# z = h @ w_in as seven products in place of eight, in two halves of the tokens, with q, k and v kept in DRAM

## The chip, the cores and the metric

The kernel runs on one core of a Trainium2 chip. A core has TensorE (PE) for matmuls, VectorE (DVE), ScalarE (ACT) and GpSimd (POOL) for work on whole tiles, and SyncE (SP), whose queue issues nearly all DMAs here. Each engine takes its own instructions in order and waits for the others by semaphores. The metric is device time in microseconds of one execution.

## What is computed

One layer of a decoder trunk over 2048 prompt tokens and 8 sample tokens, in float32. The heart is one wide product, and all branches hang on it:

```python
def _branches_in(x, c, w_c, b_c, w_in, b_in):
    mod = c @ w_c + b_c
    shift, scale, gate = jnp.split(mod, 3, axis=-1)
    h = x * (1.0 + scale[:, None]) + shift[:, None]
    z = h @ w_in + b_in
    return gate, jnp.split(z, SPLIT_POINTS, axis=-1)
...
        gate_p, (q, k, v, ga, glu, gb, ma, mb) = _branches_in(x_p, c_prompt, w_c, b_c, w_in, b_in)
...
        o_attn = _combine_groups(outs, lses)
        u = _glu(glu)
...
        conv_out = _conv_tail(u_ext, conv_w, conv_b, conv_norm_g, conv_norm_b)
...
    a = (o_attn.reshape(B, T, ATTN_OUT).astype(x.dtype) * jax.nn.silu(ga)) @ w_pa
    b = (conv_out * jax.nn.silu(gb)) @ w_pb
    y = (jax.nn.sigmoid(ma) * a + jax.nn.sigmoid(mb) * b) @ w_o
    return _layer_norm(ALPHA * x + gate[:, None] * y, ln_g, ln_b)
```

h has 1024 channels and w_in 8704 columns, 68 tiles of 128: 36 for q, k and v (12 heads of 128), 4 for the attention gate, 8 for the convolution's gated input, 4 for its gate, 16 for the merge gates. The heads stand in three groups with dilations 1, 4 and 16; a query sees its own and the previous block of keys within its residue class (group three has one block of keys only). The groups of a head slot are combined by their softmax denominators. The convolution has 31 taps per channel, then a LayerNorm. The samples attend to caches of keys and values in DRAM.

## The kernel before

**Matmuls in three parts.** w_in and h are each split into a high and a low part in a faster matmul format (ACT copies the high part, POOL or DVE subtracts it for the low part: `w_split`, lines 133 to 139, and `h_step`), and each product is high x high, high x low and low x high (`products`, line 322). The split h of all tokens stays in SBUF for the whole kernel.

**Units.** A tile of 128 columns of w_in is worked in five units of tokens, three of 512, one of 256 and one of 264 with the samples (`UNITS`, `unit`), each 24 matmuls into one PSUM bank of tag `pm` (three buffers). ACT or DVE then evacuates it (`ev_qkv`, `ev_merge`, `ev_ga`, `ev_glu`, `ev_gb`). q, k and v go to SBUF slots, permuted so that a residue class is contiguous.

**Order.** `seq` is written out by hand: one merge gate tile beside which h is made, then v, k, q head by head, an attention gate after each head slot but the last, the convolution's inputs spread among merge gates, last the convolution's gates. After most units `tick` issues what was put off, one step of a background `lane` (a generator), and steps of `conv_lane` as long as a clock kept for DVE lies behind one kept for PE. The lane holds, in turn, turning v into rows (`v_rows`), k rows for the output (`k_rows`) and `attention`: scores of a batch of blocks, mask and maximum on DVE, exponentials on ACT, turns on PE, values on PE, rows to DRAM (`orow`). These three stages are shifted by one step each, so that a step issues the values of batch s-2, the turns of s-1 and the scores of s. A step follows every 5.5 us unit, more or less. Later the lane holds the samples' attention (`s_attn`, line 886 the keys, 942 to 944 the values), the residual gate (`gate_rows`, line 971) and the convolution's norm. The combination of a head slot (`combiner`) is worked inside the units of its gate tile (`ga_tile`), two pieces at a time from four or five buffers.

**Output.** The output weights are loaded and split beneath the last two gate tiles. Then for eight chunks of tokens come the two branch products (line 1297), the merge, the product with w_o (line 1340) and the LayerNorm.

## Time and profile before

| | us |
|---|---|
| median of 3 runs | 2282.08 (2281.2 to 2283.14) |
| span of the profiled execution | 2280.6 |
| first instruction to the end of the first tile of z, about | 88.7 |
| q, k, v and attention, up to about | 1144 |
| samples, convolution, up to about | 1545 |
| remaining gates, up to | 1889.5 |
| output | 391.1 |

The page doesn't give the profiled execution's own time beside its span; the span is 1.5 us below the median of the runs. To read the rows: a matmul's duration in the trace contains its way through the array, and the next one starts before it ends, so the pace is read from start to start, or from the chain of critical work, which merges neighbours. "PE L322" is a matmul of z; "PEld" the load of its weights, which overlaps. An engine's number in a stretch is its busy time there.

### The profile page before, as it was taken

The page shows a single profiled execution, that of the slowest core. Times are in us where ns is not written, and L with a number is a line of the kernel's source. Part 1 is how long each engine was busy: PE and PEld are TensorE (multiplying, and loading weights), DVE is VectorE, ACT ScalarE, POOL GpSimd, SP SyncE. Part 2 cuts the span into 40 slices and gives each one's busy share as a digit, 9 for nine tenths or more (in the row PEclk, how much of TensorE's full clock was granted, in tenths as well). Part 3 has the DMA queues.
Part 4 walks back from the last instruction along what each step waited for, and adds up shares of the span by engine and source line. Part 5 has one row for each costly group of instructions (what it writes and reads, how often), then busy time and mean ns, then how long its engine had stood idle before and what let it go on. Part 6 is the DMA issues. An engine that isn't in the chain of part 4 may idle for free.

```text
span 2280.6 us, 30595 instructions
## 1 busy us (share of the span) xinstructions
PE 2191.2 (96%) x12633; PEld 1893.6 (83%) x12633; DVE 1038.2 (46%) x1473; ACT 625.4 (27%) x1227; POOL 529.6 (23%) x380
## 2 busy tenths in 40 slices
PE   6999999999999999999999797989999999999998
PEld 4888888888888888888888675878888888888886
DVE  4402211211512215122245999998934545554556
ACT  2323332333413334133341111221134332111110
POOL 2501001010001001010012549341122135322232
PEclk9999999999999999999999899999999999999999
DMA  7301112111320113111223532312222356334220
GB/s 255 112 21 35 39 49 56 30 34 43 120 59 22 39 50 112 53 33 39 77 87 108 157 90 78 96 52 84 70 70 80 98 185 221 110 121 130 93 95 30
DMA packets 198888, 190.16 MB, mean 83 GB/s; under 512 B 9355, under 2 KB 172991, under 8 KB 198741
## 3 DMA queue, kind: packets, MB, share of 16 engines
q1 hardware_dynamic: 198425, 187.76, 26.4%
q8 instruction: 99, 1.62, 0.3%
q10 hardware_dynamic: 324, 0.45, 0.1%
q14 instruction: 40, 0.33, 0.0%
HBM read 130.37 MB, written 58.31 MB: 83 GB/s over the span
## 4 chain that ended last, share of the span: by engine, by line
PE 75%; DVE 14%; issue 3%; DMA 1%; ACT 1%; POOL 1%; SPq 0%; POOLq 0%; DVEq 0%; ACTq 0%
PE ps_pm L322 52%; DVE slot L75 9%; PE py L1340 8%; PE pab L1297 5%; PE ps_S L433 3%; PE ps_U L473 2%; PE ps_PT L459 1%; PE ps_U L471 1%; DVE slot L71 1%; PE ps_PT L515 1%; DMA slot<-orow 1%; DVE st L1236 0%; DMA stg<-smp_d 0%; DVE ev L75 0%; DVE th L71 0%
## 5 line engine op out<-in xcount | busy, mean ns | idle before, releaser
L138 POOL TENSOR_TENSOR wL<-raw,wH 128x1024 fp32r<-128x1024 f32 x68 | 182.3, 2681 | 1150.8 <-ACT wH L137 1109.9
L322 PE MATMUL ps_pm<-h3H,wH 128*128 128x256 f32 (+1 forms) x1088 | 314.5, 289 | 0.0
L322 PE MATMUL ps_pm<-h3L,wH 128*128 128x256 f32 (+1 forms) x1088 | 309.0, 284 | 0.9 <-POOL h3L L295 0.9
L322 PE MATMUL ps_pm<-h3H,wL 128*128 128x256 f32 (+1 forms) x1088 | 307.9, 283 | 0.0
L322 PE MATMUL ps_pm<-h1H,wH 128*128 128x512 f32 x544 | 221.5, 407 | 0.0
L322 PE MATMUL ps_pm<-h2H,wH 128*128 128x512 f32 x544 | 219.4, 403 | 0.0
L322 PE MATMUL ps_pm<-h0H,wH 128*128 128x512 f32 x544 | 218.1, 401 | 0.0
L322 PE MATMUL ps_pm<-h1H,wL 128*128 128x512 f32 x544 | 215.8, 397 | 0.0
L322 PE MATMUL ps_pm<-h1L,wH 128*128 128x512 f32 x544 | 215.6, 396 | 0.0
L322 PE MATMUL ps_pm<-h2L,wH 128*128 128x512 f32 x544 | 214.3, 394 | 1.1 <-POOL h2L L295 1.1
L322 PE MATMUL ps_pm<-h0H,wL 128*128 128x512 f32 x544 | 214.1, 394 | 0.7 <-POOL wL L138 0.7
L322 PE MATMUL ps_pm<-h2H,wL 128*128 128x512 f32 x544 | 214.4, 394 | 0.0
L322 PE MATMUL ps_pm<-h0L,wH 128*128 128x512 f32 x544 | 213.5, 393 | 0.0
L83 DVE COPY Uo<-ps_U 128x256 f32<-128x256 f32 (+1 forms) x76 | 37.6, 495 | 382.0 <-PE ps_U L473 368.9
L322 PEld LDWEIGHTS ps_pm<-h3H,wH 128*128 128x128 f32 x1088 | 206.7, 190 | 5.0 <-issue 1.9
L322 PEld LDWEIGHTS ps_pm<-h3L,wH 128*128 128x128 f32 x1088 | 206.7, 190 | 3.0 <-POOL h3L L295 1.7
L322 PEld LDWEIGHTS ps_pm<-h3H,wL 128*128 128x128 f32 x1088 | 206.0, 189 | 0.0
L364 ACT ACTIVATE slot<-ps_pm,bT 128x512 f32<-128x512 f32 (+1 forms) x120 | 102.5, 854 | 313.4 <-PE ps_pm L322 312.5
L75 DVE SCALAR_TENSOR_TENSOR slot<-slot,cwT,slot 128x2048 f32<-128x2048 f32 x60 | 178.9, 2981 | 1.4
L75 DVE SCALAR_TENSOR_TENSOR slot<-u,cwT,slot 128x2048 f32<-128x2048 f32 x60 | 167.5, 2791 | 1.6
L75 DVE SCALAR_TENSOR_TENSOR X<-tab,ps_S 128x512 f32<-128x512 f32 (+1 forms) x80 | 52.3, 653 | 173.7 <-PE ps_S L433 171.9
L322 PEld LDWEIGHTS ps_pm<-h1H,wH 128*128 128x128 f32 x544 | 104.6, 192 | 22.3 <-issue 0.9
(279 smaller groups left out, 4100.7 us busy)
## 6 DMA issues: line engine op xcount, KB each, us to landing
raw<-w_in SPq DMA_DIRECT2D x68, 512.0 KB
slot<-orow SPq DMA_DIRECT2D x25, 390.0 KB
wc<-w_c SPq DMA_DIRECT2D x16, 512.0 KB
xs<-x_prompt SPq DMA_DIRECT2D x16, 512.0 KB
orow<-Uo SPq DMA_DIRECT2D x56, 130.0 KB
mrg<-tm_d SPq DMA_DIRECT2D x14, 512.0 KB
mrg<-tn_d SPq DMA_DIRECT2D x14, 512.0 KB
tm_d<-ev SPq DMA_DIRECT2D x24, 256.0 KB
```

The source lines that it names most:

```text
L71: DVE.tensor_tensor(out, a, b, op=op)
L75: DVE.scalar_tensor_tensor(out, a, s, b, op0=op0, op1=op1)
L83: DVE.tensor_copy(out, a)
L138: POOL.tensor_tensor(wL, r, f32(wH), op=OP.subtract)
L322: PE.matmul(p[:, :n], a[:, kt, :], b[c][:, kt, n0:n0 + n], start=kt == 0 and x == 0, stop=kt == KT - 1 and x == 2)
L364: ACT.activation(permuted(dst, g, c, n0, npr), src, AF.Identity, bias=bias, scale=sc)
L433: PE.matmul(S[:, s:s + w, :], Q[:, b * P:(b + 1) * P], K[:, k0:k0 + w * P], start=True, stop=True)
L459: PE.transpose(pt[:, s, :], X[:, s, :], ident)
L471: PE.matmul(U[:, n, :], Y[:, s, :], V[:, b - 1, :], start=True, stop=False)
L473: PE.matmul(U[:, n, :], Y[:, s, :], V[:, b, :], start=not prev, stop=True)
L1297: PE.matmul(p[:, :n], a, b[:, kt, :n], start=i == 0, stop=i == 11)
L1340: PE.matmul(py[h], a[:, d, c0:c0 + P], w[:, h * 512:(h + 1) * 512], start=f, stop=l)
```

## The change

Nearly the whole function is rewritten. Pairs of column tiles are worked together. Tokens fall into two halves of 1024; a half into two blocks of 512; the 1024 channels into even and odd tiles (e = 0, 1). So each pair and half is a 2 x 2 by 2 x 2 product of blocks, done in seven products by sums and differences of the blocks (on the side of h: s1 to s4, on the side of w_in: T1 to T4), with partial results shared between the four outputs.

- **Operands of h** (`OPS`, tile `A`): seven, each split in high and low, for one half of the tokens at a time; the first half's are made before z begins (`prep_first`, `prep_mod`), the second half's in the background of the first half (`prep_second`, `split_second`). In the first half a block of 512 tokens carries 4 sample columns and is worked as two pieces of 258; in the second as one of 512.
- **Operands of w_in** (`w_make`): seven for each pair of tiles and half, each 128 x 512, made by subtractions on DVE, copies on ACT and subtractions on POOL (four of seven) or DVE (three of seven). `MAKE` says after which product which operand is made. They stand in 6 buffers in the first half, 4 in the second. w_in is loaded twice.
- **Accumulation** (`quad`): the banks X (two, in turn), Y and W. ACT copies an intermediate sum out of X (c1, u2, u3) before the next product adds to it; DVE adds it at the evacuation of another output. The last two products of a pair are issued within the next pair.
- **q, k, v** go to DRAM (`zq_d`) in token order. All attention comes in the second half of the tokens, from SBUF slots loaded back head by head; the residue classes are read by stride (`blk`). `heads` is one generator for all twelve.
- **Background**: a tick after every product, in the second half also in its middle. `every` gives how often a tick steps the lane and `lane2`, which holds the combinations; these have one buffer for loaded rows and come after attention of the slot. The convolution runs by halves, each over 1024 tokens. What is left in the lanes at the end is issued after the last product.
- **Output**: its weights are loaded and split after all this, from three buffers; the rest is as before.

```diff
+OPS = ("a11", "a12", "s2", "s1", "s3", "s4", "a22")
+SUB = 258
...
+    def tiles_of():
+        def qkv(n):
+            kind, hi = "vkq"[n % 3], n // 3
+            return (kind, hi % 3, hi // 3)
+        z = [(qkv(2 * n), qkv(2 * n + 1)) for n in range(18)]
+        U = [(("ua", i, 0), ("ug", i, 0)) for i in range(4)]
+        GB = [(("gb", i, 0), ("gb", i + 1, 0)) for i in (0, 2)]
+        GA = [(("ga", i, 0), ("ga", i + 1, 0)) for i in (0, 2)]
+        M = [(("ma", i, 0), ("mb", i, 0)) for i in range(8)]
+        return [U + z + GB + GA + M, U + z[:16] + GB + z[16:] + GA + M]
...
+    def w_make(s, n):
+        def split(r):
+            t = bops[s, n] = bp.tile([P, 2, 4, P], F32R, name="bop", tag="bop", bufs=nbop[0])
+            ACT.activation(t[:, 0], r, AF.Copy)
+            split_no[0] += on_dve[0]
+            eng = POOL
+            if split_no[0] >= 7:
+                split_no[0] -= 7
+                eng = DVE
+                cost(r)
+            eng.tensor_tensor(t[:, 1], r, f32(t[:, 0]), op=OP.subtract)
...
+        if n == "b11":
+            split(R(0, 0))
+        elif n == "b21":
+            split(R(1, 0))
+            sub(R(0, 0), R(0, 1), R(0, 0))
+        elif n == "T2":
+            t2 = rw.tile([P, 4, P], F32, name="t2", tag="t2")
+            sub(t2, R(1, 1), R(0, 0))
+            split(t2)
...
+        DVE.tensor_tensor(f["s1"], F[1, 0], F[1, 1], op=OP.add)
+        DVE.tensor_tensor(f["s2"], f["s1"], F[0, 0], op=OP.subtract)
+        DVE.tensor_tensor(f["s3"], F[0, 0], F[1, 0], op=OP.subtract)
+        DVE.tensor_tensor(f["s4"], F[0, 1], f["s2"], op=OP.subtract)
+        for x, n in enumerate(OPS):
+            ACT.activation(A[n][:, 0, b], f[n], AF.Copy)
+            (DVE if x in (1, 3, 5, 6) else POOL).tensor_tensor(A[n][:, 1, b], f[n], f32(A[n][:, 0, b]), op=OP.subtract)
...
+        count[0] += 1
+        if every[0] and count[0] % every[0] == 0:
+            step(lane)
+        if every[1] and count[0] % every[1] == 0:
+            step(lane)
+        if every[2] and count[0] % every[2] == 0:
+            step(lane2)
...
+    def product(an, s, bn, acc, start, off, n, halves=False):
+        H, Lo = A[an][:, 0], A[an][:, 1]
+        w = bops[s, bn]
+        for b in range(4):
+            for x, (i, a) in enumerate(((0, H), (0, Lo), (1, H))):
+                PE.matmul(acc[:, :n], w[:, i, b, :], a[:, b, off:off + n], start=start and b == 0 and x == 0, stop=b == 3 and x == 2,
+                          skip_group_check=True)
+            clock["pe"] += 3 * (n / 2330.0 + 0.008)
+            if b == 1 and halves:
+                tick()
...
+    MAKE = ({10: (1, "b11"), 11: (1, "b21"), 13: (1, "T2"), 1: (0, "T1"), 2: (0, "T3"), 5: (0, "b22"), 7: (0, "T4")},
+            {5: (1, "b11"), 6: (1, "b21"), 0: (-1, "b22"), 1: (0, "T2"), 2: (-1, "T4"), 3: (0, "T1"), 4: (0, "T3")})
...
+            X = ps(banks[0])
+            banks.reverse()
+            product("a11", s, "b11", X, True, off, n, hv)
+            c1 = wp.tile([P, 512], F32, name="c1", tag="c1")[:, :n]
+            ACT.activation(c1, X[:, :n], AF.Copy)
+            after(s, k0)
+            Y = ps("Y")
+            product("a12", s, "b21", Y, True, off, n, hv)
+            evs[0](Y[:, :n], c1, c, sub)
+            after(s, k0 + 1)
+            if pv:
+                prev_p3(hv)
+            after(s, k0 + 2)
+            product("s2", s, "T2", X, False, off, n, hv)
+            u2 = wp.tile([P, 512], F32, name="u2", tag="u2", bufs=2)[:, :n]
+            ACT.activation(u2, X[:, :n], AF.Copy)
+            after(s, k0 + 3)
+            if pv:
+                prev_p4(hv)
+            after(s, k0 + 4)
+            W = ps("W")
+            product("s1", s, "T1", W, True, off, n, hv)
+            after(s, k0 + 5)
+            product("s3", s, "T3", X, False, off, n, hv)
+            u3 = wp.tile([P, 512], F32, name="c1", tag="c1")[:, :n]
+            ACT.activation(u3, X[:, :n], AF.Copy)
+            evs[1](W[:, :n], u3, c + 1, sub)
+            pv.update(s=s, W=W, X=X, u2=u2, evs=evs, c=c, sub=sub, off=off, n=n, done=done_fn if sub == subs - 1 else None)
+            after(s, k0 + 6)
...
+        if u is None:
+            ACT.activation(dst, a, AF.Identity, bias=bias)
+        else:
+            vstt(dst, a, bias, u, OP.add, OP.add)
...
+    def blk(t, g, b, w=1):
+
+        if g == 0:
+            return t[:, (b + 1 - w) * P:(b + 1) * P]
+        if g == 1:
+            r, c = divmod(b, 4)
+            return t[:, 512 * (c + 1 - w) + r:512 * (c + 1):4]
+        return t[:, b::16]
...
+            t = ra.tile([P, 780], F32, name="cmb", tag="cmb", bufs=ncmb[0])
+            o = t.rearrange("p (n g x) -> p n g x", n=2, g=3)
+            ld(o.rearrange("p n g x -> p n (g x)"), ov[:, 2 * i:2 * i + 2, :])
...
+        for hi in range(12):
+            g, j = hi % 3, hi // 3
+            yield from wait("v", hi)
+            yield from v_rows(g, j, sl["v"], Vn)
+            ask("v", hi + 1)
+            yield from wait("k", hi)
+            yield from wait("q", hi)
+            yield from k_rows(ra, g, j, sl["k"])
+            for _ in attention(ra, g, j, sl["q"], sl["k"], Vn, tab):
+                serve()
+                yield
+            ask("k", hi + 1)
+            ask("q", hi + 1)
+            serve()
+            if g == 2:
+                lane2.append(combine(ra, j))
...
+            if kind == "gb" and a == 2:
+                leave(f"cv{p}")
+                if p == 0:
+                    rs = enter("rs")
+                    stg = rs.tile([P, 2080], F32, name="stg")
+                    lane.append(gate_rows(rs, stg))
+                    lane.append(mark(s_attn(rs, stg), "samples"))
                 else:
+                    ra = enter("ra")
+                    lane.append(heads(ra, zdone))
+                    every[:] = [1, 0, 2]
...
+    while step(lane2):
+        flush()
+    leave("ra")
```

More of the change, by code (lines that the diff above doesn't have):

```diff
@@ L746, in u_rows @@
         yield
-    def conv(i, u):
-        if i >= 2:
-            guard("samples" if i == 2 else "gate")
-        y = ys[i] = slot((K0, K1, QS, VN)[i])
-        cw = cwT[:, i, :]
-        if i == 3:
-            lane.append(mark(conv_samples(), "csamp"))
-        vts(y[:, :L], u[:, 0:L], cw[:, 0:1], cw[:, 31:32], OP.mult, OP.add)
-        yield
-        for t in range(1, 31):
-            vstt(y[:, :L], u[:, t:t + L], cw[:, t:t + 1], y[:, :L], OP.mult, OP.add)
-            clock["dve"] += 0.12
-            yield
-        done.add(("conv", i))
```

1456 lines of the change are left out of this document (735 added, 721 removed).

## The prediction

> **What bounds the kernel now.** Read first was the page's head and then the view of stretches, cut where the critical chain changes its work: start, attention, samples and convolution, the last gates, output.
>
> ```profile
> span 2280.6 us, 30595 instructions
> ...
> PE 2191.2 (96%) x12633; PEld 1893.6 (83%) x12633; DVE 1038.2 (46%) x1473; ACT 625.4 (27%) x1227; POOL 529.6 (23%) x380
> ```
>
> ```profile
> 0.00:88.70 88.70, 69.39 (x409) 47.48 (x409) 52.35 (x73) 34.30 (x49) 42.07 (x31) 0.96 0.65 219
> 88.70:1144.00 1055.30, 1050.90 (x6119) 924.65 (x6120) 227.18 (x508) 344.55 (x765) 103.17 (x110) 1.00 0.18 51
> 1144.00:1545.00 401.00, 362.21 (x1882) 298.18 (x1881) 340.01 (x230) 80.47 (x150) 184.95 (x75) 0.95 0.32 97
> 1545.00:1889.50 344.50, 338.30 (x1892) 293.77 (x1890) 207.53 (x269) 99.16 (x162) 69.29 (x69) 1.00 0.30 100
> 1889.50:2280.60 391.10, 370.45 (x2336) 329.56 (x2336) 211.17 (x395) 66.90 (x102) 130.16 (x95) 0.99 0.34 113
> ```
>
> Each row gives length, then busy time and count of PE, weight loads, DVE, ACT, POOL, then clock, DMA share, GB/s. PE is busy nearly everywhere, at full clock; only 1144 to 1545 shows DVE nearly full (340 of 401). So removed matmuls are worth their full time, but only as long as everything that now lies beneath 5.5 us units of z still has cover. That second half decides.
>
> **What the products save.** From the critical chain, units of z in steady state:
>
> ```profile
> 1004.88 5.45 PE ps_pm L322 x24
> ...
> 1012.53 5.73 PE ps_pm L322 x48
> ```
>
> A 512-wide matmul takes 0.227 us, one of 256 or 264 columns 0.1195. Now 68 tiles x (3 x 5.45 + 5.74) = 1502 us. After: 34 pairs of tiles, each 14 products of 12 matmuls at 258 columns in the first half, 34 x 168 x 0.1195 = 683 us; in the second 34 x 84 x 0.227 = 649 us. Saving 170 us, not 188, since more of the columns run in narrow matmuls. The attention matmuls and the output stay (391 us, last row above).
>
> **The start.** The modulation's fourth block starts its turns here:
>
> ```profile
> 51.84 0.60 PE L284 MATMUL ps_S<-ident,xs 128*128 128x128 f32 x4
> ```
>
> After, as many bytes precede that point, then the block's seven operands are made (about 6 us of DVE, ACT, POOL in series), with nothing of z before it. z starts at about **58**.
>
> **First half.** Ticks (one step of background work each) come after every product, 12 x 0.1195 = 1.43 us, instead of every 5.5 us. The steps keep their own cost. For the gate rows and the samples:
>
> ```profile
> 1240.10 0.47 SPq L51 DMA_DIRECT2D stg<-smp_d  x1
> ```
>
> ```profile
> 1245.55 2.39 POOL L886 TENSOR_TENSOR slot<-slot,stg 128x1024 f32<-128x1024 f32 x1 [12.40 <-DMA stg<-smp_d]
> ...
> 1369.52 1.27 POOL L943 TENSOR_TENSOR stg<-stg 128x512 f32<-128x512 f32 x1
> 1370.87 1.59 POOL L944 TENSOR_TENSOR stg<-stg 64x512 f32<-64x512 f32 x1
> ...
> 1420.88 2.39 POOL L942 TENSOR_TENSOR stg<-stg,slot 128x512 f32<-128x512 f32 x2
> ...
> 1463.72 2.41 POOL L971 TENSOR_TENSOR slot<-stg,slot 128x1024 fp32r<-128x1024 f32 x1 [2.16 <-ACT slot L970]
> ```
>
> ```profile
> 1326.53 1.20 DVE L79 TENSOR_REDUCE slot<-slot 64x8 f32<-64x1024 f32 x1
> ```
>
> ```profile
> L137 ACT ACTIVATE wH<-raw 128x1024 fp32r<-128x1024 f32 x68 | 71.6, 1053 | 0.0
> ```
>
> Keys: load 5.45, POOL 2.39, reduce 1.20, hops 0.4: 9.4 us for each of two buffers, 4.7 per item, 12 items 56 us, for which 12 ticks hold 17 us of z. Values: POOL 5.3 us per row, 8 rows 42 us, against 11. With the store, reload, softmax and end (25) the samples take some 123 us against 43 of z and 10 of their own matmuls. PE can't run ahead: four of the seven weight operands of a pair have their low part made on POOL, in order behind these multiplies, and are made three products before use. About 78 us of waiting, with those operands' own POOL time. Gate rows: ACT 1.05, POOL 2.41, PE 0.91, hops 0.4 in a ring with one buffer, 4.8 x 8 = 38 against 11 + 7: 20. I take **100** (bounds 20, if PE gets ahead anyway, and 140, if POOL is also held up).
>
> DVE, from the chain, two timelines and the groups:
>
> ```profile
> 1459.33 4.39 DVE slot L75
> ```
>
> ```profile
> 1342.34 4.72 DVE L75 SCALAR_TENSOR_TENSOR slot<-slot,cwT,slot 128x2048 f32<-128x2048 f32 x2
> ```
>
> ```profile
> 1458.28 3.28 POOL L138 TENSOR_TENSOR wL<-raw,wH 128x1024 fp32r<-128x1024 f32 x1 [20.89 <-ACT wH L137]
> ```
>
> ```profile
> L71 DVE TENSOR_TENSOR ev<-ev,pab 128x256 f32<-128x256 f32 x56 | 23.6, 421 | 1.9
> ...
> L71 DVE TENSOR_TENSOR ev<-ev,ps_S 128x512 f32<-128x512 f32 x12 | 8.2, 685 | 9.0 <-PE ps_S L566 5.9 <-ACT slot L373 2.3 <-ACT ev L385 0.8
> ...
> L295 POOL TENSOR_TENSOR h1L<-htmp,h1H 128x512 fp32r<-128x512 f32 x6 | 8.0, 1336 | 2.0 <-ACT h1H L291 1.8
> ```
>
> A convolution tap alone takes 2.36 us, so 1.18 at half length; next to a POOL subtraction 4.39. The pacing issues some 8 taps per pair of tiles: 9.4 us, with seven subtractions of 0.59, six evacuations of 0.42 and six tiny ones 17.0 of 20.1 us. Four POOL subtractions (1.33) add 5.3 if they exclude DVE fully, 0 if not: I take 1.3 us over per pair, x 15.6 pairs = **20** (bounds 0 and 34). [...]
>
> Other PE work in this half (norm, gate, samples, second half's turns) is about **33**, norm and turns waiting on single PSUM buffers **13**. First half 683 + 33 + 13 + 20 + 100 = **849**. The turn to the second half (evacuation, sample gates, first split, in series) costs **6**.
>
> **Second half before attention**: 22.6 pairs x 19.07 = 431, norm 13. An operand is now made one product (2.73 us) ahead. For T2: evacuation 0.69, subtraction 0.59, ACT 0.53, POOL 1.34, hops 0.4 make 3.5, needed at 3.18; a tap in progress adds 0.6. About 0.9 x 20 pairs = 18, DVE's excess 7: **25** (0 to 60). Together **469**.
>
> **Attention.** It starts after the second pair of conv gates, so 11.4 pairs remain: 159 ticks, for 174 steps (15, 14 and 14 per three heads, and 2). One step's ring, from the timeline:
>
> ```profile
> 1002.52 0.38 PE L471 MATMUL ps_U<-slot,Y 128*128 128x128 f32 x2
> ...
> 1003.41 0.60 PE L459 MATMUL ps_PT<-ident,X 128*128 128x128 f32 x4
> ...
> 1003.85 0.38 PE L433 MATMUL ps_S<-slot,slot 128*128 128x256 f32 x1
> ```
>
> ```profile
> 1004.53 0.58 PE L322 MATMUL ps_pm<-h2H,wH 128*128 128x512 f32 x1
> ...
> 1004.99 0.69 DVE L75 SCALAR_TENSOR_TENSOR X<-tab,ps_S 128x512 f32<-128x512 f32 x1 [0.89 <-PE ps_S L433]
> ...
> 1007.42 0.19 ACT L451 ACTIVATION_READ_ACCUMULATOR X<-X,mz 128x1 f32 x1
> ```
>
> ```profile
> 899.63 0.69 DVE L75 SCALAR_TENSOR_TENSOR X<-tab,ps_S 128x512 f32<-128x512 f32 x1 [0.57 <-PE ps_S L433]
> ...
> 902.60 0.19 ACT L451 ACTIVATION_READ_ACCUMULATOR X<-X,mz 128x1 f32 x1
> ```
>
> ```profile
> L83 DVE COPY slot<-ps_PT 128x512 f32<-128x512 f32 x48 | 30.9, 686 | 137.4 <-PE ps_PT L515 137.4
> ```
>
> Value product 0.89, turns 0.44, scores 0.68: PE 2.01. The exponentials are ready at 1007.61, 3.08 us after the scores; with four of them (third fence, 3.16 in place of 2.62 from the first DVE operation) 3.62. Now 5.5 us of z fill that wait. After, half a product (1.36) and the value product (0.89) do: PE waits 0.8, and the ring is 3.08 + 1.12 = 4.2 us (four exponentials 4.75) in place of 3.37. Per head: first step 2.0, each batch from the second on 4.2, then 3.5 and 2.25, value rows 4 x 1.8, key rows 1.8 each: 46.2, 42.0 and 36.9 us for the three groups; four slots 500, without the last head and step 461. On top DVE's other work in a tick, ten operations per 14 ticks and a combining chain per 6 ticks, 0.95 us, of which I take 0.4 (0 to 0.95, as it falls in or out of the ring's gaps): 64. Key and query rows are loaded back (2 MB, 10 to 13 us by the rates of the first stretch and of the loads below) while value and key rows give 9: 10 (0 to 29). **535**; with no wait PE alone would need 388.
>
> **After the last product** (drain 5.5) nothing of z is left for one whole head: rows 8 x 1.3, four batches and their ends 20.7, **31**. The combining lane steps at every second tick, three steps per piece; it starts at ticks 46, 94 and 142, so 2.7 pieces of the third slot are done and 13.3 pieces remain, one buffer, one after the other:
>
> ```profile
> 574.18 4.38 SPq L51 DMA_DIRECT2D slot<-orow  x4
> ...
> 580.82 0.16 DVE L79 TENSOR_REDUCE cs<-slot 128x2 f32<-128x6 f32 x1 [7.30 <-DMA slot<-orow]
> 583.17 0.17 DVE L79 TENSOR_REDUCE cs<-slot 128x2 f32<-128x6 f32 x1 [2.19 <-DMA slot<-orow]
> ```
>
> ```profile
> 607.31 0.16 DVE L79 TENSOR_REDUCE cs<-slot 128x2 f32<-128x6 f32 x1
> ...
> 609.23 1.17 DVE L75 SCALAR_TENSOR_TENSOR slot<-slot,cs 128x128 f32<-128x128 f32 x4 [0.52 <-ACT slot L556]
> ```
>
> A load takes between 2.35 (the distance of two in a row) and 6.6 us (first in a queue); I take 4 for a lone one. The chain from first reduction to last sum is 3.1, turns and hops 0.6: 7.7 x 13.3 = **102** (81 to 137). Then the output weights, once split beneath gate tiles, are loaded with PE idle: 5.2 MB at the first stretch's 219 GB/s, **24** (10 to 30).
>
> **At nothing**: ACT's extra copies (some 8 us per 20 us pair, cover PE; 1 us per pair if they came last); four small weight loads per pair for two large, spills and reloads, all on SP, some 0.45 us each, issued a pair ahead (a late one costs a product, 2.7 us); contiguous in place of permuted evacuation, a gain of ACT only.
>
> **Sum**: 58 + 849 + 6 + 469 + 535 + 5.5 + 31 + 102 + 24 + 391 = 2470 of span against 2280.6. The page gives that execution's span; the median of the runs is 1.5 above it. So **2472**: the 170 us come back as waits.
>
> **The rivals.**
> *Cover holds (faster).* If PE gets past the samples (wait 20) and attention's ring hides but for 40 us, with DVE, T2, turn and output weights (20 + 25 + 6 + 24) at 30 in place of 75: 2472 - 80 - 107 - 45 = 2240; with all of these at nothing 2472 - 100 - 147 - 75 = 2150. For it: PE's own work is what is left at 96% now. Against: the 3.08 us gap. It decides where the tick's real wait falls under about 0.1 us.
> *Half (near or a little slower).* One of the two waits goes: 2280 to 2360.
> *Worse.* Q, K and V are now read at strides of 4 and 16 floats by PE. If that halves it, scores and turns of two groups double: per slot 11 x 0.68 + 13 x 0.44 = 13.2, 53 in all; with DVE's share in the ring at 0.8, another 64: 2590. [...]
>
> **How the numbers follow.** Forecast 0.62 (own range 2360 to 2560), cover holds 0.17, half 0.08 (0.03 of it within 0.2%, about what a measurement of this kernel can tell from no change), worse 0.13. Faster 0.17, same 0.03, slower 0.80. The range 2235 to 2610 leaves out the lower half of the first rival and the far end of the last.
>
> **What would show it.** z matmuls at 0.1195 and 0.227 us; PE waiting on POOL's low parts while the samples multiply, about 100 us; PE waits on ACT before the turns of attention, ticks of 4 us and more; a stretch of some 130 us before the output with PE nearly idle and orow loads one by one; a gap of 24 us before the first output matmul. Ticks near 3.4 us with no samples gap would make it wrong.

## The result, and the profile after

The changed kernel takes **2750.4 us** (median of 4 runs, 2748.02 to 2755.3) against 2281.6 (2279.85 to 2283.14) before on the same chip: 1.206 times, 95% interval 1.2043 to 1.2077. Slower was forecast, but 2472 us with a range up to 2610; the forecast is some 280 us short. The profiled execution took 2755.3 us, its span is 2753.5. One execution of one experiment (e12) took 3205 us at a granted clock of 0.64 and is left out below.

The head of the page after:

```profile
span 2753.5 us, 35769 instructions
...
PE 2250.9 (82%) x13041; PEld 1911.5 (69%) x13041; DVE 1613.1 (59%) x2676; ACT 842.4 (31%) x1891; POOL 710.2 (26%) x609
```

PE is busy 2251 us, 60 more than before with fewer columns to work, and stands still for 500. DVE has gone from 1038 to 1613. The view of stretches, with its columns as before (length; busy PE, weight loads, DVE, ACT, POOL; granted clock, DMA share, GB/s):

```profile
0.00:69.40 69.40, 43.69 (x229) 22.76 (x229) 44.14 (x72) 18.08 (x32) 20.07 (x32) 0.92 0.65 216
...
146.60:441.00 294.40, 275.95 (x2185) 266.04 (x2185) 268.18 (x358) 95.67 (x229) 91.84 (x54) 1.00 0.27 85
441.00:524.30 83.30, 57.03 (x413) 53.60 (x413) 47.95 (x98) 28.15 (x55) 20.95 (x35) 0.89 0.24 72
...
657.50:875.20 217.70, 128.09 (x742) 106.20 (x741) 95.57 (x141) 50.42 (x108) 109.24 (x68) 0.79 0.44 133
...
1027.70:1103.90 76.20, 47.97 (x171) 35.69 (x172) 46.16 (x51) 24.64 (x43) 24.85 (x20) 0.78 0.15 40
1103.90:1439.40 335.50, 310.76 (x1274) 240.39 (x1273) 271.52 (x280) 98.35 (x172) 96.03 (x63) 0.97 0.28 86
...
1600.00:2195.30 595.30, 513.28 (x2441) 402.54 (x2440) 297.17 (x616) 234.35 (x649) 68.42 (x116) 0.95 0.47 151
2195.30:2236.00 40.70, 26.29 (x114) 20.36 (x113) 13.39 (x20) 9.32 (x38) 0.76 (x4) 0.67 0.43 133
2236.00:2325.60 89.60, 9.10 (x26) 4.75 (x26) 33.80 (x143) 11.73 (x39) 0.00 (x0) 0.50 0.30 92
...
2339.20:2753.50 414.30, 380.67 (x2336) 336.45 (x2336) 220.93 (x398) 73.95 (x109) 142.43 (x100) 0.96 0.36 120
```

In order: the start; 13 pairs beside the convolution; 2 pairs beside its norm; 4 pairs beside gate rows and samples; the first two pairs of the second half; 15 pairs beside its convolution; 11 pairs beside attention; the last head; combining; the output. Where nothing stands beside it a pair takes 20.2 us in the first half and 19.5 to 20.1 in the second: the products cost nearly what was forecast (20.1 and 19.1); what a pair takes beyond that is waits, slowed matmuls and PE's work for the background. By the forecast's terms, cut where the first or last product of a half starts:

| us | forecast | measured | over |
|---|---|---|---|
| start | 58 | 69 | 11 |
| first half (34 pairs, products alone 683) | 849 | 958 | 109 |
| turn and second half up to 1598 (products 431) | 475 | 570 | 95 |
| attention up to the last product | 540.5 | 597 | 57 |
| last head | 31 | 41 | 10 |
| combining | 102 | 90 | -12 |
| output weights and output | 415 | 428 | 13 |

The first half's 109 are beside the convolution 13 (33 over the products measured, 20 forecast), its first three pairs 17 (26.6, 28.2 and 22.4 us; none forecast), the norm some 22, and gate rows, samples and what follows them some 55.

### The profile page after: what moved, and what is told of

Same layout as the page of the kernel before. It is cut to its first block, busy times and chain, and to the rows that moved or that the text cites. A ratio compares the mean times of both kernels' runs of the same rounds, so it can differ in the third digit from the quotient of the medians.

```text
span 2753.5 us, 35769 instructions
## 1 busy us (share of the span) xinstructions
PE 2250.9 (82%) x13041; PEld 1911.5 (69%) x13041; DVE 1613.1 (59%) x2676; ACT 842.4 (31%) x1891; POOL 710.2 (26%) x609
## 5 line engine op out<-in xcount | busy, mean ns | idle before, releaser
L209 POOL TENSOR_TENSOR bop<-raw,bop 128x512 fp32r<-128x512 f32 x239 | 352.3, 1477 | 1165.5 <-ACT bop L202 1127.5
L427 PE MATMUL ps_W<-As,bop 128*128 128x258 f32 (+1 forms) x2448 | 460.9, 337 | 82.3 <-DVE sga L77 36.4
L427 PEld LDWEIGHTS ps_W<-As,bop 128*128 128x128 f32 x2448 | 374.7, 199 | 136.6 <-issue 41.5
L77 DVE SCALAR_TENSOR_TENSOR y<-u,cwT,y 128x1024 f32<-128x1024 f32 x240 | 357.6, 1490 | 3.5
L202 ACT ACTIVATE bop<-raw 128x512 fp32r<-128x512 f32 x408 | 251.1, 622 | 46.5 <-DVE raw L73 44.0
L427 PE MATMUL ps_X<-As,bop 128*128 128x258 f32 (+1 forms) x1224 | 238.4, 342 | 32.2 <-ACT bop L202 24.8
L427 PE MATMUL ps_Z<-As,bop 128*128 128x258 f32 (+1 forms) x1224 | 228.5, 334 | 11.9 <-POOL bop L209 8.4
L427 PE MATMUL ps_X<-Aa,bop 128*128 128x258 f32 (+1 forms) x1224 | 225.8, 333 | 12.4 <-ACT bop L202 10.3
L427 PE MATMUL ps_Y<-Aa,bop 128*128 128x258 f32 (+1 forms) x1224 | 226.2, 333 | 8.3 <-ACT bop L202 4.7
L427 PE MATMUL ps_Z<-Aa,bop 128*128 128x258 f32 (+1 forms) x1224 | 224.6, 333 | 0.0
```

What stands on the lines that cost most here:

```text
L77: DVE.scalar_tensor_tensor(out, a, s, b, op0=op0, op1=op1)
L202: ACT.activation(t[:, 0], r, AF.Copy)
L209: eng.tensor_tensor(t[:, 1], r, f32(t[:, 0]), op=OP.subtract)
L427: PE.matmul(acc[:, :n], w[:, i, b, :], a[:, b, off:off + n], start=start and b == 0 and x == 0, stop=b == 3 and x == 2, skip_group_check=True)
```

## The experiments

Each is the changed kernel with one edit or a few (the diffs show the core; buffer counts change with some), timed beside the kernel before, which took 2279.7 to 2284.4 us there. "Pair" is the time of as many matmuls of z as a pair has, 168 in the first half and 84 in the second, counted from the start of the half. Where an edit doesn't touch a stretch it still differs by up to 7 us between runs (the stretch from the norm to the second half takes 473 to 480 us in seven of them). The changed kernel's pairs, for comparison: 22.6 beside the first convolution, 54.6, 59.4, 67.5 and 36.2 beside gate rows and samples, 22.4 beside the second convolution, 51 to 57 beside attention.

### The stride: e1

```diff
-            return t[:, 512 * (c + 1 - w) + r:512 * (c + 1):4]
-        return t[:, b::16]
+            return t[:, (b + 1 - w) * P:(b + 1) * P]
+        return t[:, b * P:(b + 1) * P]
```

> Changed: the blocks of groups 2 and 3 are read as 128 neighbouring columns instead of columns 4 or 16 apart, so scores, key rows and value rows of these groups are of other tokens (computation changed). Theory A, the stride costs PE time and that time is in the ring of a step: the scores of a batch go from 1.5 (stride 4) and 1.6 us (stride 16) back to 0.68 and 0.81, value turns lose 0.1 to 0.3 each; per slot of three heads 7 x 0.82 + 4 x 0.8 + about 4 = 13 us, for 11 heads before the last product some 45: the run takes 2700 to 2715. Rival B, the tick is set by the exponentials or by DVE, so a shorter score only lengthens a wait: 2740 to 2755, with the waits before the turns longer by what the scores lost. Rival C, the long scores are not from the stride but from matmuls of z in between: their rows stay at 1.5 us.

2725.3 us: 25 less, 22 of it in the last twelve pairs (595 us for 617). The timeline of PE, the score matmuls of a batch at stride 16 and at stride 4 in the changed kernel and then in this one (start, duration, engine, line):

```profile
1735.58 1.99 PE L997 MATMUL ps_S<-sl_k,sl_q 128*128 128x128 f32 x8
...
1842.27 2.09 PE L997 MATMUL ps_S<-sl_k,sl_q 128*128 128x256 f32 x4
```

```profile
1717.33 1.06 PE L997 MATMUL ps_S<-sl_k,sl_q 128*128 128x128 f32 x8
...
1825.59 1.03 PE L997 MATMUL ps_S<-sl_k,sl_q 128*128 128x256 f32 x4
```

The groups by line, in the stretch beside attention, changed kernel and e1 (busy time, mean ns of one, idle time before them):

```profile
L997 PE MATMUL ps_S<-sl_k,sl_q 128*128 128x256 f32 (+1 forms) x352 | 113.7, 461 | 0.0
...
L1023 PE MATMUL ps_PT<-ident,X 128*128 128x128 f32 x284 | 68.1, 307 | 29.5 <-ACT X L1015 24.4
```

```profile
L997 PE MATMUL ps_S<-sl_k,sl_q 128*128 128x256 f32 (+1 forms) x352 | 80.2, 362 | 0.2 <-DMA sl_q<-zq 0.2
...
L1023 PE MATMUL ps_PT<-ident,X 128*128 128x128 f32 x284 | 68.7, 310 | 37.2 <-ACT X L1015 32.4
```

The granted clock is 1.00 around both rows of the changed kernel. Six 512-wide matmuls of z take 1.72 us behind its first row and 1.73 behind e1's second. At a stride a batch of scores takes twice as long (1.99 for 1.06 us, 2.09 for 1.03), so rival C is out. The scores lose 33.5 us, the waits before the turns gain 8: theory A's cause, with a quarter hidden as B says; the total is 10 us above A's range. Whether it is the queries (the side loaded as weights) or the keys was not tried; both are strided here.

### The ring of a step, and the value rows' bank: e2, e6, e12

```diff
-        for s in range(n + 2):
-            if 0 <= s - 2 < n:
-                s_pv(s - 2)
-            if 0 <= s - 1 < n:
-                s_tr(s - 1)
+        for s in range(n + 3):
+            if 0 <= s - 3 < n:
+                s_pv(s - 3)
+            if 0 <= s - 2 < n:
+                s_tr(s - 2)
```

> Changed: the turns of a batch come two steps after its scores instead of one, the value product three instead of two (X has 3 buffers, the slope table and the combining gates 1). Nothing is left out. Theory A, the tick is the ring scores - exponentials - turns: the waits of PE before the turns (61 us in the stretch 1600 to 2195) go, a tick falls from 3.8 to about 3.4, the stretch from the first attention step to the last product loses 60 to 80 us. Against that stand 11 more steps which find no product and combining that starts later, some 40 us after the last product: 2710 to 2735 in all. Rival B, PE's own work with strided reads, the one buffer of the value rows and DVE set the tick: the stretch loses under 20 us, and the run is 2760 to 2785.

2729.9 us (2724.33 to 2735.37). The row of the turns, in the same view:

```profile
L1023 PE MATMUL ps_PT<-ident,X 128*128 128x128 f32 x256 | 39.7, 277 | 0.3 <-ACT X L1015 0.3
```

The wait for the exponentials is gone and the last twelve pairs (from 1577.6 in the changed kernel) take 567 us in place of 617. After the last product come 31 us more. Theory A, though 50 us is less than its 60 to 80.

```diff
-            pt = ps("PT", (P, 4, P))
+            pt = ps(("PT", "U")[i % 2], (P, 4, P))
```

> Changed: the four turns of value rows of a head use two PSUM banks in alternation (PT and U) instead of PT alone. Nothing is left out. Theory A, PE waits at these turns for the copy out of the one bank (23.5 us of idle time before the turns of v in the stretch 1600 to 2195, 21.7 before those of k): the waits before v fall to under 8 us: 2725 to 2740. Rival B, the copy is late because DVE is busy with the batches before it, so the same wait turns up one turn later: 2745 to 2755.

2733.8 us, 17 less, 12 of it in the attention pairs (605 for 617): between the two. The rest lies in pairs that the edit doesn't touch.

> Changed: the turns of attention one step later, value rows in two banks, and groups 2 and 3 read 128 neighbouring columns (other tokens, computation changed). Theory A, in the changed kernel the stride was partly hidden in the ring; with the ring gone its time counts in full (33 us between the busy times of the scores, some 10 for the turns): 20 + 17 + 40 us less, 2670 to 2680, and the ten full attention pairs take 42 to 46 us each instead of 53. Rival B, DVE or PE's own 44 us per pair is the limit: the three gains don't add, 2695 to 2720.

2703.3 us, from one execution. The twelve pairs take 546 us, 71 less, where the three single edits took 50 + 22 + 12 = 84: the gains nearly add, so no other limit stands close behind. But 26 us come back after the last product, so the total falls in rival B's range although the pairs speak for theory A.

### DVE, POOL and the late operand: e3, e5, e8

```diff
-        for t in range(1, 31):
+        for t in range(1, 2):
```

> Left out: 29 of the 30 further taps of the convolution of prompt tokens (DVE, 1.49 us each, 232 in all). [...] Rival B, in the second half the pair is late because its operands are made only one product before use: there pairs stay at 21.5 or more, and the run takes 2700 to 2715.

2669.8 us: 81 less. Pairs fall to 20.2 in the first half and to 20.05 in the second, under rival B's 21.5, and the run is under its range. Beside the convolution a subtraction on POOL takes 1.40 us in place of 1.73. e8 takes rival B up again.

```diff
-    on_dve = [3]
+    on_dve = [7]
```

> Changed: all seven low parts of a pair's weight operands are made on DVE; before, four of seven on POOL. Nothing is left out. Theory A, a subtraction on POOL and a DVE operation with two SBUF inputs shut each other out: beside the convolution a tap takes 1.50 us instead of 1.18 and a raw difference 1.40 instead of 0.69, so four POOL subtractions of 1.73 cost DVE as much as they last (some 7 us per pair), while four more subtractions on DVE cost 2.8. Taps fall to 1.15 to 1.25, pairs in the convolution from 22.6 to 20.2 us in the first half (-33) and from 22.4 to 20 to 20.5 in the second (-30), and in the samples' stretch low parts no longer queue behind POOL's multiplications, but behind DVE's reductions (0 to -20): 2665 to 2695. Rival B, the engines only share bandwidth and DVE has the more to do: taps stay at 1.4 or more, pairs rise to 24 to 25 us: 2790 to 2810.

The groups of DVE and POOL beside the first convolution, changed kernel (two rows of DVE, one of POOL), then e5 (DVE):

```profile
L77 DVE SCALAR_TENSOR_TENSOR y<-u,cwT,y 128x1024 f32<-128x1024 f32 x101 | 151.0, 1495 | 1.2
L73 DVE TENSOR_TENSOR raw<-raw 128x512 f32<-128x512 f32 x26 | 36.5, 1403 | 7.1 <-POOL bop L209 7.1
...
L209 POOL TENSOR_TENSOR bop<-raw,bop 128x512 fp32r<-128x512 f32 x52 | 89.5, 1730 | 195.4 <-ACT bop L202 195.3
```

```profile
L77 DVE SCALAR_TENSOR_TENSOR y<-u,cwT,y 128x1024 f32<-128x1024 f32 x83 | 106.1, 1278 | 0.3
...
L73 DVE TENSOR_TENSOR raw<-raw 128x512 f32<-128x512 f32 x27 | 18.5, 685 | 0.0
```

With POOL out of the way a tap takes 1.28 in place of 1.50 us, a raw difference 0.69 in place of 1.40, and pairs run at 20.2 to 20.8 and 19.5 although DVE has four more subtractions in each: theory A. The means of the changed kernel mix two cases: a tap that meets no POOL subtraction takes 1.28 us, others up to 2.36. One that starts 0.10 us behind a POOL subtraction of 1.33 us (at 220.20) takes 2.31, a raw difference that starts 1.21 us ahead of the end of two of them in a row (3.58 us from 207.86) takes 1.76, and an evacuation out of a bank beside one more (zst<-ps_Y at 216.27) takes 0.48, its mean. Yet the run takes 2741.0 us, only 9 less. The slower paced convolution ends later: the norm falls into the stop ahead of the conv gates, where all that is left is issued at once (77.4 us for one pair in the second half, where the norm's dearest pair took 47.8), and attention's twelve pairs take 637 us in place of 617.

```diff
-            {5: (1, "b11"), 6: (1, "b21"), 0: (-1, "b22"), 1: (0, "T2"), 2: (-1, "T4"), 3: (0, "T1"), 4: (0, "T3")})
+            {4: (1, "b11"), 5: (1, "b21"), 6: (0, "b22"), 0: (0, "T2"), 1: (-1, "T4"), 2: (0, "T1"), 3: (0, "T3")})
...
-            nbop[0] = 4
+            nbop[0] = 5
```

> Changed: in the second half each weight operand is made one product earlier (two ahead of its use; five buffers instead of four, and four small tiles with fewer buffers). Nothing is left out. [...] Rival B, the short lead is what the convolution's DVE work hits: pairs fall from 22.4 to 20: 2690 to 2715.

2698.3 us, 52 less: rival B. PE's waits for weight operands in the changed kernel's 15 pairs, the longest two groups (in all, times, longest):

```profile
PE ps_Z L427 <- POOL bop L209: 7.3, 6, 1.7
PE ps_X L427 <- POOL bop L209: 6.4, 6, 1.6
```

In e8 no such wait is listed there, and twelve of the 15 pairs take 19.5 to 19.9 us each (21.9 on average before). The first three take 81 us in place of 72.5; PE waits there 14.0 us for rows of the convolution's input (4.5 before). The stretch before attention loses 44 us in all. In the second half DVE's full use alone holds nobody; the operand made one product ahead comes late when a tap (1.50 us on average there) or a POOL subtraction (1.52 and 1.73) holds DVE. Taking away the taps, POOL or the short lead each removes the same 2.3 to 2.9 us per pair.

### Gate rows and samples: e4, e9, e10, e16, e18

```diff
                     lane.append(mark(s_attn(rs, stg), "samples"))
+                    every[:] = [2, 0, 0]
...
-            if p == 0 and n == 29:
+            if p == 0 and n == 30:
...
                 leave("rs")
+                every[:] = [1, 0, 0]
```

> Changed: between the last conv gates and the end of the sample attention the background lane steps after every second product instead of every one, and the samples may end one pair of tiles later. Nothing is left out. Theory A, a step of the samples or gate rows costs its own chain (load, multiplication, reduction, some 4.7 to 5.3 us) less the products that run meanwhile, as PE's evacuations and low parts stand behind it in the order of DVE and POOL: with two products per step the 137 us that four pairs lost fall to 40 to 70: 2670 to 2690. Rival B, the loads and POOL's work have to be waited for whatever the pace: the loss is only spread over more pairs, 2735 to 2755.

2718.1 us. From the norm's end to the second half there are 303 us of products; the changed kernel takes 479.7, this one 439.0. A gain between the two forecasts.

```diff
-        return [U + z + GB + GA + M, U + z[:16] + GB + z[16:] + GA + M]
+        return [U + z[:15] + GB + z[15:] + GA + M, U + z[:16] + GB + z[16:] + GA + M]
...
+                    every[:] = [3, 0, 0]
```

> Changed: in the first half the conv gates come after 15 of the 18 pairs of q, k, v instead of after all, so that gate rows and samples (44 steps) start earlier, and they step after every third product; the sample attention waits for the last q, k, v pair and may end one pair later. Nothing is left out. Theory A, a step of this lane takes about 4.8 us from its load to its end whatever the pace (four pairs of 217.7 us for 44 steps; every second product made it 49 half ticks in 236 us, 4.8 again), so the loss is 44 times what the products between two steps leave of it: with three products (4.3 us) it falls from 146 us to 30 to 50: 2635 to 2665. Rival B, a good part of it is the lane's own PE work and DVE and POOL being full, which no pace removes: loss 80 to 100 as with two products, 2690 to 2715.

2704.6 us, the stretch 428.5, still 125 over its products: theory A, 4.8 us per step whatever the pace, falls; the total is rival B's.

```diff
-        every[:] = [1, 0, 0]
+        every[:] = [2, 0, 0]
         for n, pair in enumerate(quads[p]):
```

> Changed: until the conv gates of each half the background lane (samples of the convolution, its norm) steps after every second product instead of every one. Nothing is left out. Theory A, the norm's steps are chains over PE, DVE, POOL and ACT of 2 to 3 us, and a product of 1.4 us does not cover one: the 43 us lost in the first half and the 29 in the second fall by about half: 2705 to 2725. Rival B, the norm's work fills DVE and ACT, whatever the pace: 2740 to 2755, the loss spread over twice the pairs.

2696.1 us. In the first half the setting stays in force to its end, so the run contains e4's pace as well (which theory A's total does not) and is to be compared with that: 22 us less. The four pairs at the norm take 113 us (127 in the changed kernel), three in the second half 83 (88). Most of the norm's loss is only spread.

Then the loads were moved four items ahead, on top of e4:

```diff
-        nxt = [k_load(0), k_load(1)]
+        nxt = [k_load(i) for i in range(4)]
...
-            t = (y3, stg)[b % 2][:, 0:1536].rearrange("p (g x) -> p g x", g=3)
+            t = (y3, y4, s4, stg)[b % 4][:, 0:1536].rearrange("p (g x) -> p g x", g=3)
```

> The run with every second product, and besides: four buffers in place of two for the samples' keys, queries and values, loads four items ahead, a value row collected two steps after its multiplication. Nothing is left out. With three products per step the loss did not fall to 30 to 50 us; PE still waits for bank W, which DVE empties in order behind the key reductions, these wait for POOL, and POOL for a load (DVE waits of up to 11.0 us). PE's slack for a held-up DVE is about 4 us (of inserted work of 2.8, 6.9 and 15.2 us nothing, 2.8 and 11.5 reached it). Theory A, the holds of DVE by late loads are what comes through: with loads four items ahead they go, and the stretch from the norm to the second half falls from 439 to 385 to 405 us (303 are products, some 30 PE's other work): 2665 to 2685. Rival B, POOL's own time and PE's waits for gate rows and loads of x are what is left: 420 or more, 2700 to 2718.

2715.4 us, stretch 435.5, the same as e4's 439.0 within what runs differ by: loads further ahead gain nothing. Last, on top of this, no low part on POOL during the samples, and a key item reduced one step later:

```diff
+            reduce_last(i)
             POOL.tensor_tensor(kk, kk, qq, op=OP.mult)
-            vred(SC[:NKEY[g], g, 8 * b2:8 * b2 + 8], kk.rearrange("p (r d) -> p r d", d=P), OP.add)
+            last.append((g, b2, kk))
...
                     every[:] = [2, 0, 0]
+                    on_dve[0] = 7
```

> The run with loads four items ahead, and besides, while gate rows and samples run: all low parts of weight operands on DVE (none on POOL), and the reduction of a key item one step after its multiplication. Nothing is left out. Theory A, the hold is a ring through engines that work in order: PE waits for DVE to empty bank W, DVE's reduction stands before that and waits for POOL's multiplication, which stands behind a low part, which waits for ACT's high part, which stands behind a copy out of the bank that PE fills next. With no low part on POOL and no reduction that waits for the step it belongs to, the ring is cut: the stretch from the norm to the second half falls from 436 to 385 to 405 us, the run to 2670 to 2690. Rival B, the ring isn't the cause, and what is left is PE's waits for gate rows, for x, and slow matmuls behind them: 420 or more, 2695 to 2715.

2700.1 us, stretch 427.4: rival B's numbers again. The view of waits, of the changed kernel's four sample pairs, and of PE in e18 over nearly the whole stretch (in all, times, longest):

```profile
PE ps_W L427 <- DVE sga L77: 36.4, 3, 14.0
...
POOL y L758 <- DMA stg<-smp_d: 32.9, 7, 20.3
DVE y L81 <- POOL y L758: 32.9, 7, 11.0
```

```profile
PE ps_W L427 <- DVE smg L77: 28.7, 8, 9.1
...
PE ps_S L928 <- DMA x<-x_prompt: 11.2, 4, 4.9
```

PE waits for DVE to empty the one bank W in both. In the changed kernel DVE is held by key reductions, these by POOL's multiplications, and those by loads of the samples' queries; the longest wait (14.0) contains the first of them, where DVE waits 11.0 us. That first load is issued one step before its use, behind six stores in SP's queue, in e16 and e18 too, so the edit moved only the later ones. What stands before the evacuation that ends e18's longest wait (9.1, until 760.46):

```profile
750.14 2.37 POOL L770 TENSOR_TENSOR y<-y,stg 128x1024 f32<-128x1024 f32 x1 [38.37 <-DMA stg<-smp_d]
752.54 1.22 DVE L81 TENSOR_REDUCE y<-y 128x8 f32<-128x1024 f32 x1 [4.76 <-POOL y L770]
...
755.19 0.79 DVE L209 TENSOR_TENSOR bop<-raw,bop 128x512 fp32r<-128x512 f32 x1 [0.97 <-ACT bop L202]
...
755.90 2.82 DVE L73 TENSOR_TENSOR raw<-raw 128x512 f32<-128x512 f32 x1
758.65 1.21 DVE L81 TENSOR_REDUCE y<-y 128x8 f32<-128x1024 f32 x1
```

The first load again; then the low part that the edit moved to DVE, which waits for ACT, a raw difference that takes 2.82 us beside a multiplication on POOL (in the changed kernel 2.85, at 759.59, 0.32 us behind a multiplication of 2.63), and one more reduction. The edit changed what holds DVE and didn't free it. An earlier first load and a second bank W were not tried.

### What a wait costs: e13

```diff
+        if p == 0 and k == 5 and 19 <= stream[s][1] <= 21:
+            for _ in range((4, 10, 22)[stream[s][1] - 19]):
+                DVE.tensor_scalar(probe_y[0], probe_y[0], 1.0, None, op0=OP.mult)
```

> Added: in three pairs of the first half that run undisturbed (20.2 us each, after the norm and before the conv gates) DVE multiplies a convolution row by 1.0 in place 4, 10 and 22 times (some 0.6 to 1.2 us each) just before a product whose evacuation PE needs. Nothing is left out. Theory A, a wait of PE is charged twice: the products behind it run at half clock for some us (after a wait of 9.8 us in another run's sample stretch two products took 2.7 and 2.2 us instead of 1.43), so the two longer waits cost their idle time and 2 to 4 us more, the short one only its idle time. Rival B, slow matmuls there come from something else in that stretch (loads, POOL): here each pair is longer by its idle time alone, within 0.5 us.

One execution, 2772.7 us. An inserted operation takes 0.69 us. The three pairs take 20.2, 24.7 and 33.7 us. PE's timeline around the second wait, then the third:

```profile
575.79 1.60 PE L427 MATMUL ps_Y<-Aa,bop 128*128 128x258 f32 x12
580.15 2.92 PE L427 MATMUL ps_W<-As,bop 128*128 128x258 f32 x12 [2.76 <-DVE sv L77]
582.87 1.89 PE L427 MATMUL ps_Z<-As,bop 128*128 128x258 f32 x12
584.59 1.61 PE L427 MATMUL ps_X<-Aa,bop 128*128 128x258 f32 x12
```

```profile
613.56 2.92 PE L427 MATMUL ps_W<-As,bop 128*128 128x258 f32 x12 [11.50 <-DVE sq L77]
616.27 2.20 PE L427 MATMUL ps_Z<-As,bop 128*128 128x258 f32 x12
618.31 1.61 PE L427 MATMUL ps_X<-Aa,bop 128*128 128x258 f32 x12
```

Four operations (2.8 us) cost nothing, so PE has some 4 us of slack for a held-up DVE here: ten (6.9) become 2.76 of waiting, 22 (15.2) become 11.5. Behind either wait twelve matmuls take 2.7 us from start to start instead of 1.44, and the next ones some 0.3 to 0.6 too long. The pairs lose 4.5 and 13.5 us for 2.76 and 11.5 of idle time: **each of the two waits costs its idle time and 1.7 to 2.0 us more**. Theory A, at the lower end of its price or a little below. The view of stretches shows why (the clock is the third number from the end):

```profile
580.10:583.50 3.40, 3.35 (x15) 3.38 (x16) 1.60 (x4) 0.90 (x2) 0.00 (x0) 0.50 0.22 77
613.50:617.60 4.10, 4.04 (x19) 4.07 (x20) 1.83 (x5) 0.91 (x2) 0.00 (x0) 0.50 0.18 64
```

The granted clock is 0.50 for the first 3.4 and 4.0 us of work behind the two waits; half of that time is the 1.7 and 2.0 us lost, and from 584.59 and 618.31 on twelve matmuls take 1.45 us again. Among the gate rows of the changed kernel the clock is 1.00 behind four waits of 1.73 and 1.74 us and for 1.3 us behind a last one of 2.17, then 0.50 from 710.7 to 714.0 and 1.00 again:

```profile
709.38 0.39 PE L860 MATMUL ps_S<-hl,cHL 128*9 128x512 f32 x1 [2.17 <-POOL hl L846]
...
710.07 2.29 PE L427 MATMUL ps_Y<-Aa,bop 128*128 128x258 f32 x12
712.16 2.46 PE L427 MATMUL ps_W<-As,bop 128*128 128x258 f32 x12
714.46 1.61 PE L427 MATMUL ps_X<-As,bop 128*128 128x258 f32 x12
```

Counting all matmuls of z whose distance to the next is 1.4 to 2.6 times the median one: 459 of 5651 in the first half, 42.8 us too long together, and 271 of 2678 in the second, 51.4: 94 us. In the kernel before the same count gives 26.

### The tail: e7

```diff
-    ncmb = [1]
+    ncmb = [2]
```

> Changed: the rows to be combined have two buffers (the next load starts before the chain of this one) and a piece takes two steps instead of three; to make room the slope table and three small tiles have fewer buffers. Nothing is left out. Theory A, after the last product a piece costs its load and its chain in series (7.0 us, 13 pieces, 89.6 us): with the load hidden 3.5 to 4 us remain, and one or two more pieces are done before the last product: the stretch falls to 40 to 50 us, the run to 2700 to 2712. Rival B, the chain over DVE, ACT and PE is itself 6 us or more: the stretch stays over 75 us, 2735 to 2750.

2735.2 us. PE's timeline at two pieces, changed kernel and e7:

```profile
2239.47 0.74 PE L1124 MATMUL ps_S<-ident,cmb 128*128 128x128 f32 x2 [3.52 <-DVE cmb L77]
2246.47 0.74 PE L1124 MATMUL ps_S<-ident,cmb 128*128 128x128 f32 x2 [6.26 <-DVE cmb L77]
```

```profile
2290.79 0.69 PE L1124 MATMUL ps_S<-ident,cmb 128*128 128x128 f32 x2 [3.38 <-DVE cmb L77]
2294.84 0.69 PE L1124 MATMUL ps_S<-ident,cmb 128*128 128x128 f32 x2 [3.36 <-DVE cmb L77]
```

A piece takes 4.05 us in place of 7.0 and three fewer are left; what follows the last product shrinks from 559 to 512 us, as theory A says. But the last product ends 30 us later, so only 15 us are kept and the total is rival B's. The three more pieces worked beside attention are the likely reason; whether the smaller buffers have a share was not tried.

### Light background: e14, e15

The core of the edit in both (scores, exponentials and turns go as well):

```diff
-            vcopy(Uo[:, :nb, :P], U[:, :nb, :])
-            POOL.tensor_copy(Uo[:, :nb, P:P + 2], mz[:, :nb, :])
+            POOL.memset(Uo[:, :nb, :], 1.0)
...
-        for t in range(1, 31):
+        for t in range(1, 2):
...
-            POOL.tensor_tensor(kk, kk, qq, op=OP.mult)
```

> The changed kernel with a light background. Left out: scores, exponentials, turns and value products of attention (each batch stores a constant instead), 29 of 30 further taps of the convolution, the samples' multiplications and key reductions. Loads, value and key rows, norm, gate rows, combining and output stay. Theory A, cover: these chains are what PE waits for, so beside PE's own 153 us for 76 batches and 33 us of strided reads also their waits go (attention about 100, convolution 84, samples 60, the last head 25): about 2290, and the distance to the kernel before with the same things left out shrinks from 469 to 100 to 190 us. Rival B, the halves themselves (turn, operands one product ahead, slow clock, tail) carry the loss: 2400 or more, distance above 300.

> The kernel before with the same things left out as in the changed kernel with the light background: attention's batches, 29 of 30 further taps, the samples' multiplications and reductions. Theory A, its waits were covered by 5.5 us units, so hardly more goes than PE's own work: 153 us of 76 batches and some 25 of the 39 us in which PE stood still between 1144 and 1545: 2095 to 2115. Rival B, hidden waits were in it too: 2060 or less.

2389.3 and 2066.8 us. The distance shrinks from 469 to 322 us only: rival B's distance for the changed kernel (its time is 11 us under B's 2400), and for the kernel before a value between the two, nearer to B. The stretch beside what is left of attention in the first, and steady units in the second:

```profile
1449.00:1845.00 396.00, 304.86 (x1290) 236.43 (x1290) 180.26 (x405) 115.22 (x231) 85.90 (x120) 0.91 0.75 236
```

```profile
88.70:1000.00 911.30, 910.26 (x5018) 790.05 (x5017) 109.91 (x341) 228.81 (x358) 118.01 (x113) 1.00 0.22 61
```

PE stands still for 1 us in 911 there, for 91 in 396 here, with loads now at a DMA share of 0.75. So removing the long chains is not enough. In that stretch PE waits 27.0 us for combining, 43.5 for the copies of value and key rows and 12.3 for their loads; norm and gate rows wait too. And 541 us follow the last product in the first, against 397 after the last gate in the second: 144 of the 322.

### All gains together: e11, e17

The edits of e2, e6 and e8 with the paces of e9 and e10, then with the loads of e16 in place of e9's pace.

> Changed, all together: gate rows after every second and samples after every third product with the conv gates after 16 pairs of q, k, v; the norm after every second product; weight operands of the second half one product earlier; the turns of attention one step later; value rows in two banks; to make room one buffer instead of two for four small tiles, two instead of three for evacuated rows. Nothing is left out. If the waits are separate, their gains add: 2750 - 100 (samples) - 35 (norm) - 52 (earlier operands) - 20 (later turns) - 17 (two banks) = about 2525. If they stand in for one another (a product that no longer waits for its operand waits for an evacuation), 2560 to 2610. In either case slower than before by 10% or more: the turn of the halves, the ring of what is left and the stretches after the last product stay.

2613.0 us, 1.145 times the kernel before (1.1433 to 1.1471). By stretches, in the traces: first half 51 less, second half before attention 44, attention 79, after the last product 30 more. The single runs gave 55 (e10), 44 (e8), 50 and 12 (e2, e6) and 31 more (e2) in the same stretches: the gains don't stand in for one another, but the samples' 100 were never there, and the time is outside both forecasts.

> Everything together that took time off: loads of the samples four items ahead and every second product, the norm after every second product, operands of the second half one product earlier, later turns in attention, value rows in two banks, smaller buffers to make room. Nothing is left out. By the stretches of the single runs: first half 958 - 60 to 95, second half before attention 550 - 44, attention 617 - 79, after the last product 559 + 30: 2565 to 2600. Theory A (loads ahead count): at the lower end. Rival B: 2600 to 2615, as without them.

2612.9 us, 1.144 (1.1418 to 1.1469), rival B: loads further ahead add nothing to it. No version that computes everything beats the kernel before.

## Why the prediction missed

**Right**: the direction and its ground. The products cost nearly what the rows of before said, and the saving of 170 us comes back as waits. Attention's ring is real (e2), combining is a serial chain of load and work (7.0 us a piece, 7.7 forecast), DVE and POOL hold each other up (e5: without POOL's subtractions a tap takes 1.28 us for 1.50, a raw difference 0.69 for 1.40; e3: with one further tap left a subtraction on POOL takes 1.40 for 1.73), the operand made one product ahead is late (e8).

**The step that failed** is the sum of the waits, in four terms:

- *The second half before attention*, 25 us for late operands and a turn of 6. Measured over the products 49.5 beside the convolution (3.3 us per pair, 1.3 forecast), 38 at the turn and 29 at the norm (13 forecast). The forecast took the taps as an addition of at most 0.6 us to an operand's chain; e8 shows that one more product of lead removes PE's waits for operands there. At the turn PE waits once for 19.5 us for a high part on ACT, a queue that the forecast priced at one split:

```profile
PE ps_X L427 <- ACT bop L202: 21.4, 2, 19.5
```

- *The first half*. 275 us beyond the products against 166. For the samples 100 were forecast, with PE held by low parts behind POOL's multiplications. The size was some 55 us short and the reason wrong: in the changed kernel's four pairs PE waits 2.0 us for a low part on POOL and 36.4 for the evacuation of bank W, and with no low part on POOL (e5) they still took 55.0, 55.1, 66.2 and 36.1. What PE waits for is DVE, whose reductions stand behind the multiplications and their loads. The waits of the norm were priced at 13 us together with those of the second half's turns, and the first pairs at nothing; the norm took 43 us beyond its products, some 22 more than its share, and the first three pairs 17.
- *Attention*. The stride was placed in a rival, as doubling scores and turns, a supposition that no row of the forecast shows. It doubles the scores (e1) and takes 22 us of the attention pairs, not the rival's 53 for scores and turns: the ring hides part of it, and the turns of value rows change little (mean 305 and 294 ns). The forecast's row for one bank of value rows (1.8 us a turn) missed that the copy queues behind DVE's other work (e6: 12 to 17).
- *The clock*. Every product was priced at full speed and every wait at its idle time. 94 us of slow product matmuls stand in the trace, 68 more than before; in e13 such matmuls come behind the two waits (twelve in 2.7 us for 1.44, at a granted clock of 0.50) and not in the pair without one (20.2 us). It is a quarter of the miss and lies in all other terms.

## What to carry to other kernels

Count what the removed matmuls were covering before counting what they cost: each background step here needs its own chain of several engines, and a product of 1.4 or 2.7 us covers what one of 5.5 covered only if the operand, the bank and the step are each a product or two further ahead. Price waits of PE like the two measured here (2.76 and 11.5 us) at their length plus some 2 us (1.7 and 2.0). Where one engine's queue holds both the evacuations and the background, a cure in one stretch (fewer operations there, more pieces beside) is often paid in the next, so read every stretch again after each.

## What the runs showed of the hardware that was not expected

- Scores whose queries and keys are read at strides of 4 or 16 floats take about twice the time: four 256-wide matmuls at stride 4 2.09 in place of 1.03 us, eight 128-wide ones at stride 16 1.99 in place of 1.06.
- The granted clock was 0.50 for the first 3.4 and 4.0 us of work behind waits of PE of 2.76 and 11.5 us (e13). Behind one of 2.17 us (changed kernel, at 709.38) it was 1.00 for 1.3 us and then 0.50 for 3.35 us; behind four waits of 1.73 and 1.74 us before it, 1.00.
- A DVE difference of two 128x512 tiles takes 0.69 us with nothing on POOL (e5), 1.40 on average beside the first convolution with POOL's subtractions (1.73 each there), and 2.82 (e18) and 2.85 (changed kernel) in two cases beside POOL's multiplications.
